# Linear attention: the sample states' stores and row fetches queued behind the small tokens' weight requests, their scaled copies behind an eviction

## Chip, cores and metric

One core of a Trainium2 chip runs the kernel. The metric is the device time of one execution in microseconds (us), as the median of several runs. The engines are PE (TensorE matmuls), PEld (its weight loads), DVE (VectorE), ACT (ScalarE), POOL (GpSimd) and SP (SyncE, which here only issues DMAs).

## What is computed

One inference step of a two-layer trunk: gated linear attention (GLA) with an MLP, then differential attention with an MLP, on 1024 prompt tokens, 16 meta tokens and 8 running sequences with one new token each. The change lies in the first layer, in what the 8 running sequences ("samples") need. For each sample b and each of 4 heads the state of 128 x 256 numbers is updated as

```
q, k, v, lg, r = gla_project(x, w_in, w_gate, b_gate)
new_state = exp(lg)[..., None] * state + k[..., None] * v[..., None, :]
o = q @ new_state
```

and the new states (8 samples of 512 KB) are an output, `gla_state_s`. The samples' and the meta tokens' rows ("small tokens", 24 rows padded to 32) also go through the output projection, the norms, the MLP of layer 1 and the projection of layer 2; the small tokens' results are needed later by the second layer.

## The kernel before

**Prompt.** The projections of the prompt are split-precision matmuls (`mm3`, L205 to L208: three matmuls on high and low parts of both sides). Weights come as 256 KB pieces (`unit`, L191), are cast by ACT (L193, high part) and POOL (L194, low part). For each head h, `proj(h)` (L370 to L392) makes q and k (four accumulations, evicted by ACT at L313/L315) and v (four accumulations, evicted by ACT at L391 into `Y`), `decays` (L435) builds the decay factors with many small ACT (L405 to L407, L419, L420) and DVE (L418, L423, L424) instructions and small matmuls (L452, L467), and `advance` (L494) carries the state from block to block (L500 to L504). While the decays of head 1 are made, PE already works on the projections of head 2.

**Small tokens.** `small_tokens` (L789) is a generator. Each step first uses the two weight tiles of 1 MB that the step before requested (`sload` L234 or `sload2` L240, both from the pool `swt` of two buffers), in 16 matmuls (L722 or L733), and then requests the next two, as soon as the matmuls have freed the buffers. There are 24 such pairs. After the first two pairs, those of the output projection (`gla_w_out`), `s_post` (L736) copies the sums out of PSUM on ACT (L741, "the sums' eviction"), transposes them on PE (L744) and runs a chain of about 15 small operations that ends with the new `sx` (L777); the pairs of the MLP follow, whose matmuls need that `sx`. The function `deal` (L829) advances the generator by one step.

**Sample states.** `state_updates` (L653) is a second generator, with 8 rounds n. In a round, `fetch` (L661) requests a 512 KB broadcast row of v into a part of `Y` (L665) and, for rounds 5 to 7, a 512 KB state (L646); `outer` (L672) scales that row on ACT by k, four instructions (L674); `update` (L667) does decay and sum on DVE, four instructions (L670); `store` (L676) writes the state back (L678). The rows lie in `Y[:, 4096:7168]`, where heads 2 and 3 later put their v.

**Order.** The instructions are not issued in the order of the program text: a planner goes through a simulated timeline and puts on each engine's queue the ready instruction that stands first in the program. The order on each engine is then fixed, and an engine waits in order. `tc.issue_after(x)` makes the instructions inside the block come after x on x's engine; it adds no wait of its own. `swl` is a list of weight requests, which before the change only `sload2` fills; L644 to L646 uses its entry `w_in`. The loop at L834 to L848 advances `updates` by one round after every accumulation of `proj`, and `small` after every second one.

Of the kernel before, what the change touches and what calls it, by code (L numbers as in the profile page):

```python
# [15 lines left out]
AF = mybir.ActivationFunctionType  # L16
# [9 lines left out]
NM = 16  # L26
NS = 8
TS = 32
GH = 4
# [85 lines left out]
def hybrid_step(ctx, tc, A, dbg=None, upto=9):  # L115
    nc = tc.nc
    V, S, G, TE = nc.vector, nc.scalar, nc.gpsimd, nc.tensor
    dma = nc.sync.dma_start
# [23 lines left out]
    def mmt():  # L142
        return banks["mm"].tile([P, 512], F32, name="mmt") if "mm" in banks else pairt()[:, 0]
# [4 lines left out]
    def smt():  # L148
        return banks["sm"].tile([P, 512], F32, name="smt")
# [75 lines left out]
    def s2():  # L225
        return s2p.tile([P, 512], F32, name="s2")

    def swt():
        return swp.tile([P, 2, D], F32, name="swt")

    def sload(src):

        t = swt()
        dma(t.rearrange("p k n -> p (k n)"), src)  # L234
        return t.rearrange("p k n -> p (k n)")

    def sload2(w, k, eng=None):
# [5 lines left out]
    swl = []  # L243
# [99 lines left out]
    ps = smt()  # L343
# [16 lines left out]
    ps = smt()  # L360
# [9 lines left out]
    def proj(h):  # L370
        hi, lo = qku if h == 0 else qk_unit(h)
        hv, lv = (w.rearrange("p (i k n) -> p i k n", i=2, n=P) for w in (hi, lo))
        for c in range(h == 0, 2):
            cs = slice(512 * c, 512 * c + 512)
            for i in range(2):
                ps = mmt()
                for k in range(NB):
                    mm3(ps, hv[:, i, k, :], lv[:, i, k, :], XH[:, k, cs], XL[:, k, cs], k == 0, k == NB - 1)
                evict_qk(c, i, ps)
                yield  # L380
        hi, lo = v0u if h == 0 else kunit(wi, 1024 + h * 256)
        hv, lv = (w.rearrange("p (k n) -> p k n", n=256) for w in (hi, lo))
        for c in range(2):
            for i2 in range(2):
                ps = mmt()
                for i in range(2):
                    t = 4 * c + 2 * i2 + i
                    for k in range(NB):
                        a = slice(t * P, (t + 1) * P)
                        mm3(ps[:, i * 256 : (i + 1) * 256], XH[:, k, a], XL[:, k, a], hv[:, k, :], lv[:, k, :], k == 0, k == NB - 1)  # L390
                S.copy(Yh[:, h, 4 * c + 2 * i2 : 4 * c + 2 * i2 + 2, :].rearrange("p i e -> p (i e)"), ps)  # L391
                yield  # L392
# [37 lines left out]
    def gate_in(h, c):  # L430
        pg = axt()
        TE.matmul(pg, wg[32 * c : 32 * c + 16, h * P : (h + 1) * P], gT[32 * c : 32 * c + 16, :], start=True, stop=True)
        return pg
# [79 lines left out]
    def state_out():  # L513
        h, st = ends.pop()
        dma(A["gla_state_p"][0, 0, h], st)

    def head_end(h, st):
        ends.append((h, st))
        rr = rstd_of(gss[:, h, :], 8, 1.0 / 256, g2)
        G.tensor_tensor(Yh[:, h], Yh[:, h], bc(rr, [P, 8, 256], 2), op=ALU.mult)  # L520
# [42 lines left out]
    ps = smt()  # L563
# [4 lines left out]
    ps = smt()  # L568
# [5 lines left out]
    skT = sqk[:, 128:].rearrange("p (h t) -> p h t", t=TS)  # L574
    V.tensor_scalar(sqT, pv[:, 0], P ** -0.5, None, ALU.mult)
    V.tensor_copy(skT, pv[:, 1])
    ps = smt()
# [15 lines left out]
    ps = smt()  # L593
# [5 lines left out]
    for hh in range(2):  # L599
        ps = smt()  # L600
        for i in range(2):
            h = 2 * hh + i
# [11 lines left out]
    ps = smt()  # L614
# [4 lines left out]
    for s in (8, 4, 2, 1):  # L619
        u = t2()[:, :128]  # L620
        level(sb.rearrange("p h t -> p (h t)"), sqk[:, :128], sqk[:, 128:], u, s, V)
        ps = smt()
# [17 lines left out]
    def slot(i):  # L640
        t = Y[:, 5120 + 1024 * i : 6144 + 1024 * i] if i < 3 else st2[:, i - 3, :]
        return t.rearrange("p (h e) -> p h e", e=256)

    def state_in(b, i):  # L644
        with tc.issue_after(w_in):
            dma(slot(i), A["state_gla"][0, b].rearrange("h d e -> d h e"))  # L646

    for b in range(NS):
        state_in(b, b % 5)
        for h in range(GH):  # L650
            TE.matmul(po[h * TS : (h + 1) * TS, :256], qmk[:, h, b, :], slot(b % 5)[:, h, :], start=False, stop=b == NS - 1)

    def state_updates():  # L653

        todo = ((5, 0), (6, 1), (7, 2), (3, 3), (4, 4), (0, 3), (1, 4), (2, 3))

        def vb(n):
            at = 4096 if n < 2 else 4096 + 1024 * (1, 0, 2)[(n - 2) % 3]
            return Y[:, at : at + 1024].rearrange("p (h e) -> p h e", e=256)

        def fetch(n):  # L661
            b, i = todo[n]
            if b < 3:
                state_in(b, i)
            dma(vb(n).rearrange("p h e -> p (h e)"), A["vs"][b : b + 1, :].broadcast_to([P, D]))  # L665

        def update(n):  # L667
            b, i = todo[n]
            for h in range(GH):
                V.scalar_tensor_tensor(slot(i)[:, h, :], slot(i)[:, h, :], ses[:, h, b : b + 1], vb(n)[:, h, :], ALU.mult, ALU.add)  # L670

        def outer(n):  # L672
            for h in range(GH):
                S.activation(vb(n)[:, h, :], vb(n)[:, h, :], AF.Copy, scale=skT[:, h, NM + todo[n][0] : NM + todo[n][0] + 1])  # L674

        def store(n):  # L676
            b, i = todo[n]
            dma(A["gla_state_s"][0, b].rearrange("h d e -> d h e"), slot(i))  # L678

        last = len(todo) - 1  # L680
        fetch(0)
        outer(0)
        for n in range(last + 1):
            yield
            if n:
                store(n - 1)
                if n < last:
                    fetch(n + 1)
                outer(n)
            update(n)  # L690
            if n == 0:
                fetch(1)
        yield
        store(last)
        yield
# [11 lines left out]
    ps = smt()  # L707
# [28 lines left out]
    def s_post(ps, ln, pool):  # L736

        sev = ps
        if pool is spool:
            sev = s2()  # L740
            S.copy(sev, ps)  # L741
        pt = smt()
        for j in range(4):
            TE.transpose(pt[:, j * P : (j + 1) * P], sev[:, j * P : (j + 1) * P], ident)  # L744

        pv = pt.rearrange("p (j q c t) -> p q c j t", j=4, q=2, c=2)
        z = pool.tile([P, NB, TS], F32, name="sz")
        for c in range(2):
            zc = z[:, 4 * c : 4 * c + 4, :]
            V.scalar_tensor_tensor(zc, sx[:, 4 * c : 4 * c + 4, :], ALPHA, pv[:, 0, c], ALU.mult, ALU.add)  # L750
            V.tensor_tensor(zc, zc, pv[:, 1, c], op=ALU.add)
        s_ln(z, ln, pool)

    def s_ln(z, ln, pool):
        s1 = pool.tile([P, TS], F32, name="ss1")
        V.tensor_reduce(s1, z.rearrange("p k t -> p t k"), op=ALU.add, axis=AX.X)
        pm = smt()
        TE.matmul(pm[:, :TS], inv, s1, start=True, stop=True)
        V.tensor_tensor(z, z, bc(pm[:, :TS], [P, NB, TS], 1), op=ALU.subtract)
        z2 = s2()[:, : NB * TS].rearrange("p (k t) -> p k t", t=TS)  # L760
        V.tensor_tensor(z2, z, z, op=ALU.mult)
        V.tensor_reduce(s1, z2.rearrange("p k t -> p t k"), op=ALU.add, axis=AX.X)
        pm = smt()
        TE.matmul(pm[:, :TS], inv, s1, start=True, stop=True)
        v = pool.tile([P, TS], F32, name="sv_")
        y = pool.tile([P, TS], F32, name="sy_")
        V.tensor_scalar(v, pm[:, :TS], EPS, None, ALU.add)
        S.activation(y, v, AF.Ln)
        S.activation(y, y, AF.Exp, scale=-0.5)

        V.tensor_tensor(v, v, y, op=ALU.mult)
        V.tensor_tensor(v, v, y, op=ALU.mult)
        V.tensor_scalar(v, v, -0.5, 1.5, ALU.mult, ALU.add)
        V.tensor_tensor(y, y, v, op=ALU.mult)
        V.tensor_tensor(z, z, bc(y, [P, NB, TS], 1), op=ALU.mult)
        V.tensor_tensor(z, z, bc(lnp[:, ln, 0, :], [P, NB, TS], 2), op=ALU.mult)
        V.tensor_tensor(sx, z, bc(lnp[:, ln, 1, :], [P, NB, TS], 2), op=ALU.add)  # L777
# [11 lines left out]
    def small_tokens():  # L789
# [35 lines left out]
        dma(A["sxd"], sx)  # L825

    small, updates = small_tokens(), state_updates()

    def deal():  # L829
        next(small, None)  # L830
# [3 lines left out]
    for h in range(1, GH):  # L834
        for n, _ in enumerate(proj(h)):
            if n == 1:
                state_out()
            next(updates, None)
            if n % 2:
                deal()  # L840
        st = SM[:, h, :]
        pgs = [gate_in(h, c) for c in range(2)]
        for c in range(2):
            parts = decays(h, c, pgs[c])
            if c or h == 1:
                deal()
            st = advance(h, c, st, *parts)
        head_end(h, st)  # L848
# [3 lines left out]
    for h in range(GH):  # L852
# [3 lines left out]
        for c in range(2):  # L856
            cs = slice(512 * c, 512 * c + 512)
            sil, pts = [], []
            for m in range(2):
                ps = mmt()  # L860
# [390 lines left out]
    for u, t2_ in ((u, t) for u in range(12) for t in range(4)):  # L1251
# [6 lines left out]
        ps = mmt()  # L1258
        for i in range(2):
            t = 2 * t2_ + i  # L1260
# [139 lines left out]
    ps = smt()  # L1400
# [34 lines left out]
    heads, vals, todo = {0: head}, {0: load_v(0)}, []  # L1435
    steps = [(h, n, t) for h in range(8) for n, t in enumerate((3, 2, 1, 0, 7, 6, 5, 4) if h == 7 else (7, 1, 5, 3, 6, 0, 4, 2))]
    for step in steps + [None] * 0:
        if step:
            h, n, t = step
# [93 lines left out]
    def samples():  # L1533

        sev = s2()
        dma(sev, A["srow"])
        s_post(sev, 2, hp)
        yield
# [282 lines left out]
```

## Time and profile before

| | |
|---|---|
| median of 3 runs | 2797.39 us (2790.05 to 2799.0) |
| the profiled execution's own time | 2801.98 us |
| its span, first to last instruction | 2800.2 us |
| PE busy | 2718.8 us, 97% |
| PEld busy | 2231.4 us, 80% |
| DVE, ACT, POOL busy | 69%, 40%, 38% |
| read from HBM, written | 533.00 MB, 29.52 MB |

The profile shows one execution. "Busy" of an engine counts its instructions, not the waits between them; the time an engine sits idle stands in brackets behind the instruction that ended the idle time, with what released it. PE's instructions overlap a little, and their ends are modelled, so that only its idle times are read here as lost.

### The profile page before, as it was taken

The numbers are of one execution on the slowest core, as the hardware profiler recorded it, in microseconds if no ns is written. First come the engines' busy times: TensorE is split into PE (matmuls) and PEld (weight loads), VectorE is DVE, ScalarE is ACT, GpSimd is POOL, SyncE is SP. The second block draws the span as 40 slices with busy tenths as digits, with TensorE's granted clock in tenths as the row PEclk, the third lists the DMA queues.
The fourth block names the chain that finished last, engine by engine and source line by source line (L and its number), as shares of the span: only waits on it lengthen the run. The fifth ranks groups of instructions, "written<-read, shape, count | busy, mean of one in ns | idle before, by whom it ended". The sixth has DMA issues, their size and how long they took to land. (4 is left out here: it accounts for less than half of the span.)

```text
span 2800.2 us, 52282 instructions
## 1 busy us (share of the span) xinstructions
PE 2718.8 (97%) x19849; PEld 2231.4 (80%) x19849; DVE 1920.3 (69%) x3000; ACT 1125.6 (40%) x2316; POOL 1069.8 (38%) x736
## 2 busy tenths in 40 slices
PE   8999999999999999999999999899999999999998
PEld 5877767987777777777798989777899889798986
DVE  5355453578887777777667730887647878988687
ACT  4354463152231222221242112777626536355554
POOL 2112212334344443434233312200026666676765
PEclk9999999999999999999999999999999999999999
DMA  7575645735898898888658995212144564654575
GB/s 236 166 243 198 216 150 184 262 99 182 294 326 320 313 347 306 329 318 306 252 170 313 366 361 176 66 54 76 35 126 89 104 152 101 144 118 101 137 182 120
DMA packets 276392, 562.81 MB, mean 201 GB/s; under 512 B 23510, under 2 KB 144412, under 8 KB 272044
## 3 DMA queue, kind: packets, MB, share of 16 engines
q1 hardware_dynamic: 256076, 522.75, 54.1%
q0 software_dynamic: 20064, 36.71, 8.1%
q8 instruction: 156, 2.56, 0.4%
q14 instruction: 96, 0.79, 0.1%
HBM read 533.00 MB, written 29.52 MB: 201 GB/s over the span
## 5 line engine op out<-in xcount | busy, mean ns | idle before, releaser
L194 POOL TENSOR_TENSOR wlo<-raw,whi 128x512 fp32r<-128x512 f32 x252 | 365.3, 1463 | 729.1 <-ACT whi L193 643.3
L206 PE MATMUL mmt<-whi,XH 128*128 128x256 f32 (+1 forms) x1760 | 523.9, 300 | 1.1 <-DVE ast L1348 0.9
L207 PE MATMUL mmt<-wlo,XH 128*128 128x256 f32 (+1 forms) x1760 | 521.5, 297 | 0.4 <-POOL wlo L194 0.4
L206 PE MATMUL mmt<-XH,whi 128*128 128x512 f32 (+1 forms) x1216 | 434.5, 359 | 7.2 <-DVE HL L203 2.4
L208 PE MATMUL mmt<-whi,XL 128*128 128x256 f32 x1536 | 432.0, 284 | 0.0
L208 PE MATMUL mmt<-XH,wlo 128*128 128x512 f32 (+1 forms) x1216 | 431.8, 356 | 0.2 <-POOL wlo L1645 0.2
L193 ACT CAST whi<-raw 128x512 fp32r<-128x512 f32 x252 | 150.1, 619 | 567.0 <-PE mmt L208 186.1
L206 PEld LDWEIGHTS mmt<-whi,XH 128*128 128x128 f32 x1760 | 330.2, 188 | 38.8 <-issue 23.5
L953 DVE TENSOR_REDUCE sc<-pg 128x16 f32<-128x1024 f32 x256 | 308.3, 1211 | 68.5 <-POOL pg L952 66.0
L207 PEld LDWEIGHTS mmt<-wlo,XH 128*128 128x128 f32 x1760 | 331.7, 189 | 18.1 <-issue 7.9
L207 PE MATMUL mmt<-XL,whi 128*128 128x512 f32 x768 | 306.7, 400 | 0.0
L952 DVE TENSOR_TENSOR pg<-pg,qb 128x1024 f32<-128x1024 f32 x192 | 265.7, 1391 | 56.7 <-DMA pg<-in_cache_k 49.8
L208 PEld LDWEIGHTS mmt<-whi,XL 128*128 128x128 f32 x1536 | 288.0, 189 | 5.5 <-issue 5.0
L206 PEld LDWEIGHTS mmt<-XH,whi 128*128 128x128 f32 x1216 | 228.8, 189 | 54.3 <-issue 10.8
L952 POOL TENSOR_TENSOR pg<-pg,qb 128x1024 f32<-128x1024 f32 x64 | 162.0, 2533 | 253.8 <-DMA pg<-in_cache_k 159.3
L208 PEld LDWEIGHTS mmt<-XH,wlo 128*128 128x128 f32 x1216 | 229.1, 188 | 34.8 <-issue 2.5
L206 PE MATMUL mmt<-whi,HH 128*128 128x512 f32 x512 | 204.8, 401 | 5.0 <-DVE Y L1185 3.5
L208 PE MATMUL mmt<-whi,HL 128*128 128x512 f32 x512 | 203.9, 398 | 0.0
L207 PE MATMUL mmt<-wlo,HH 128*128 128x512 f32 x512 | 203.4, 397 | 0.0
L1645 POOL TENSOR_TENSOR wlo<-rw,whi 128x512 fp32r<-128x512 f32 x92 | 153.4, 1745 | 88.3 <-ACT whi L1644 88.3
L1645 POOL TENSOR_TENSOR wlo<-RW,whi 128x512 fp32r<-128x512 f32 x96 | 160.5, 1715 | 67.7 <-ACT whi L1644 65.7
L207 PEld LDWEIGHTS mmt<-XL,whi 128*128 128x128 f32 x768 | 145.0, 189 | 38.7 <-issue 7.2
(450 smaller groups left out, 5678.2 us busy)
## 6 DMA issues: line engine op xcount, KB each, us to landing
pg<-in_cache_k SPq DMA_DIRECT2D x256, 512.0 KB
pg<-in_cache_v SPq DMA_DIRECT2D x256, 512.0 KB
raw<-in_mlp_w SPq DMA_DIRECT2D x164, 256.0 KB
swt<-in_mlp_w SPq DMA_DIRECT2D x32, 1024.0 KB
rw<-in_mlp_w SPq DMA_DIRECT2D x116, 256.0 KB
RW<-in_mlp_w POOLq DMA_DIRECT2D x96, 256.0 KB, 5.8
swt<-in_gla_w_in SPq DMA_DIRECT2D x12, 1024.0 KB
swt<-in_diff_w_in SPq DMA_DIRECT2D x12, 1024.0 KB
```

The source lines that it names most:

```text
L193: S.copy(hi[:, c], raw)
L194: G.tensor_tensor(lo[:, c], raw, hi[:, c].bitcast(F32), op=ALU.subtract)
L206: TE.matmul(ps, ah, bh, start=first, stop=False)
L207: TE.matmul(ps, ah, bl, start=False, stop=False)
L208: return TE.matmul(ps, al, bh, start=False, stop=last)
L952: eng.tensor_tensor(pg, pg, qb, op=ALU.mult)
L953: return V.tensor_reduce(sc[:, n, :], pg.rearrange("p (h d) -> p h d", d=64), op=ALU.add, axis=AX.X).ins
L1645: G.tensor_tensor(lo[:, k, :], t, hi[:, k, :].bitcast(F32), op=ALU.subtract)
```

## The change

Three edits. `sload` now also notes its request in `swl`, so that `swl[-1]` is always the latest weight request of the small tokens. In a round of `state_updates` the store and the next fetch are put behind `swl[-1]` on SP, and from the first eviction of `s_post` on, the scaled copies of `outer` are put behind the latest such eviction on ACT. In the loop over the heads `deal` now comes before `next(updates)`.

```diff
     def sload(src):
         t = swt()
-        dma(t.rearrange("p k n -> p (k n)"), src)
+        swl.append(dma(t.rearrange("p k n -> p (k n)"), src).ins)
         return t.rearrange("p k n -> p (k n)")
...
+    evicted = []
+
     def state_updates():
...
         def outer(n):
-            for h in range(GH):
-                S.activation(vb(n)[:, h, :], vb(n)[:, h, :], AF.Copy, scale=skT[:, h, NM + todo[n][0] : NM + todo[n][0] + 1])
+            with tc.issue_after(evicted[-1]) if evicted else nullcontext():
+                for h in range(GH):
+                    S.activation(vb(n)[:, h, :], vb(n)[:, h, :], AF.Copy, scale=skT[:, h, NM + todo[n][0] : NM + todo[n][0] + 1])
...
             if n:
-                store(n - 1)
-                if n < last:
-                    fetch(n + 1)
+                with tc.issue_after(swl[-1]):
+                    store(n - 1)
+                    if n < last:
+                        fetch(n + 1)
                 outer(n)
...
         if pool is spool:
             sev = s2()
-            S.copy(sev, ps)
+            evicted.append(S.copy(sev, ps).ins)
...
             if n == 1:
                 state_out()
-            next(updates, None)
             if n % 2:
                 deal()
+            next(updates, None)
```

## Rows read from the trace of the kernel before

**Rows 1.** The page: span, and busy time of each engine.
```profile
span 2800.2 us, 52282 instructions
PE 2718.8 (97%) x19849; PEld 2231.4 (80%) x19849; DVE 1920.3 (69%) x3000; ACT 1125.6 (40%) x2316; POOL 1069.8 (38%) x736
```
**Rows 2.** Busy time in three stretches: stretch, its length, PE, PEld, DVE, ACT, POOL, clock, DMA.
```profile
0.00:140.00 140.00, 131.78 (x1234) 98.75 (x1235) 64.63 (x154) 59.86 (x145) 26.21 (x24) 0.99 0.62 201
140.00:560.00 420.00, 402.31 (x3773) 314.10 (x3773) 213.25 (x412) 174.00 (x410) 91.48 (x55) 0.99 0.60 209
560.00:2800.00 2240.00, 2184.71 (x14847) 1818.54 (x14845) 1642.43 (x2435) 891.77 (x1761) 952.13 (x657) 0.99 0.63 200
```
**Rows 3.** PE in order of time, 160 to 420 us; idle before and its releaser in brackets.
```profile
162.49 1.92 PE L722 MATMUL smt<-swt,soT 128*32 128x512 f32 x16
180.25 1.92 PE L722 MATMUL smt<-swt,soT 128*32 128x512 f32 x16 [2.44 <-DMA swt<-in_gla_w_out]
189.61 0.91 PE L744 MATMUL smt<-c_ident,s 128*128 128x128 f32 x4 [2.41 <-ACT s L741]
213.84 1.92 PE L733 MATMUL smt<-swt,sx 128*32 128x512 f32 x16
221.77 0.70 PE L501 MATMUL axt<-gS,t 128*128 128x256 f32 x2 [1.67 <-DVE gS L504]
236.92 1.92 PE L733 MATMUL smt<-swt,sx 128*32 128x512 f32 x16 [1.74 <-DMA swt<-in_mlp_w]
283.50 1.92 PE L733 MATMUL smt<-swt,sx 128*32 128x512 f32 x16 [1.28 <-DMA swt<-in_mlp_w]
415.01 1.12 PE L501 MATMUL axt<-gS,t 128*128 128x256 f32 x2 [3.01 <-DVE gS L504]
```
**Rows 4.** SP's DMA issues in order of time, 160 to 230 us.
```profile
160.40 3.28 SPq L665 DMA_DIRECT2D Y<-vs  x2
167.65 0.39 SPq L678 DMA_DIRECT2D out_gla_state_s<-Y  x1
168.13 0.46 SPq L665 DMA_DIRECT2D Y<-vs  x1
168.64 2.06 SPq L240 DMA_DIRECT2D swt<-in_gla_w_out  x2
...
181.78 2.78 SPq L646 DMA_DIRECT2D st<-in_state_gla  x2
184.61 0.97 SPq L234 DMA_DIRECT2D swt<-in_mlp_w  x2
...
214.97 0.34 SPq L234 DMA_DIRECT2D swt<-in_mlp_w  x1
...
227.97 1.20 SPq L234 DMA_DIRECT2D swt<-in_mlp_w  x2
```
**Rows 5.** ACT in order of time, 175 to 223 us.
```profile
175.10 1.71 ACT L674 ACTIVATE Y<-Y,sqk 128x256 f32<-128x256 f32 x4 [5.31 <-DMA Y<-vs]
...
183.74 1.70 ACT L674 ACTIVATE Y<-Y,sqk 128x256 f32<-128x256 f32 x4
...
187.80 1.29 ACT L674 ACTIVATE Y<-Y,sqk 128x256 f32<-128x256 f32 x3
188.99 0.56 ACT L741 COPY s<-smt 128x512 f32<-128x512 f32 x1
...
222.41 0.57 ACT L391 COPY Y<-mmt 128x512 f32<-128x512 f32 x1
```
**Rows 6.** DVE in order of time: the states' updates of two rounds.
```profile
162.63 5.00 DVE L670 SCALAR_TENSOR_TENSOR Y<-Y,ses 128x256 f32<-128x256 f32 x4 [1.56 <-ACT Y L674]
...
188.76 1.67 DVE L670 SCALAR_TENSOR_TENSOR st<-st,ses,Y 128x256 f32<-128x256 f32 x4
```
**Rows 7.** Busy time and granted clock in two stretches around 190 us (columns as rows 2).
```profile
180.00:200.00 20.00, 16.87 (x162) 11.98 (x163) 19.52 (x44) 12.10 (x33) 3.40 (x3) 0.91 1.01 358
190.00:193.00 3.00, 3.00 (x16) 2.22 (x15) 3.00 (x5) 2.44 (x7) 2.45 (x2) 0.50 0.99 404
```

## The prediction, made before the changed kernel was run

> **What bounds the kernel now.** I read the page first. Its list of busy times says that PE is busy for 2718.8 of 2800.2 us, and no other engine for more than 69% [rows 1]. So PE's queue sets the time, and a change elsewhere can gain only what it takes out of PE's idle time, which is 2800.2 - 2718.8 = 81.4 us in all. The second view is the busy time by stretches. The change touches nothing before 140 us, and the small tokens, which it serves, are done by 560 us; in that stretch PE is busy for 402.31 of 420 us [rows 2]. The gain is thus bounded: 17.7 us of idle time, plus what a lowered clock takes from busy time.
>
> The third view is PE in order of time, to see which waits make up these 17.7 us. Two large ones lie next to each other, and both belong to the small tokens [rows 3]. At 180.25 us PE has sat idle for 2.44 us until the second pair of output-projection weights landed. At 189.61 us it has sat idle for 2.41 us until ACT had copied the sums out of PSUM (L741). [...]
>
> The fourth view, SP in order of time, tells why the pair was late. The first pair's matmuls run from 162.49 us for 1.92 us, so the buffers are free at 164.4 us [rows 3]. The request for the second pair leaves SP only at 168.64 us, right behind a store at 167.65 and a row fetch at 168.13 us [rows 4]. That store waited for a state update on DVE, which ran from 162.63 for 5.00 us, until 167.63 us [rows 6]. SP waits in order, so 4.2 us of the pair's delay come from the store in front of it. The fifth view, ACT in order of time, tells why the copy was late: four scaled copies at 183.74 us (1.70 us) and three at 187.80 us (1.29 us) stand in front of it, and it starts at 188.99 us [rows 5], although its matmuls had ended at 180.25 + 1.92 = 182.2 us [rows 3].
>
> **The change, part by part.** *Requests on SP.* Under the new rule sit 7 stores, 6 row fetches and 3 state loads, 16 DMAs; the last store is not under it. None is added or removed. The first of them that matter are the store at 167.65 and the row at 168.13 us: both now come behind the second pair. That pair can leave at about 164.5 us. From request to use it took 180.25 - 168.64 = 11.6 us; a later pair with less beside it took 236.92 - 227.97 = 8.95 us [rows 3, 4]. It lands at 173.5 to 176.1 us by these two, and PE asks for it at 180.25 - 2.44 = 177.8 us. At either end the 2.44 us are gone. I take the whole. What SP holds back in exchange is the stores and rows themselves, which wait for the pair's buffers; nobody on PE waits for a store.
>
> The third pair (184.61 us, behind two state loads that held SP for 2.78 us [rows 4]) also leaves earlier, by up to 2.4 us, but its matmuls at 213.84 us [rows 3] wait for the new `sx`, and with no idle time in front, so I cost it at nothing. If `sx` came so early that the weights were last, the cost would be what the pair is late, 0 to 1.74 us as at 236.92 us [rows 3].
>
> *Scaled copies on ACT.* The rounds from the first eviction on, 3 to 7, now stand behind it: 20 instructions, about 0.43 us each (1.70 for four). Without the seven in front of it the eviction would end at 188.99 + 0.56 - 1.70 - 1.29 = 186.6 us; PE asks for it at 189.61 - 2.41 = 187.2 us, so the 2.41 us go [rows 3, 5]. If only the three at 187.80 us leave, it ends at 188.3 us and 1.1 us of the wait stays: the part is worth 1.3 to 2.41 us, and I take 2.41, since both groups belong to rounds behind the eviction.
>
> *The copies come later, and the updates with them.* Rounds 3 to 5 move into the stretch where DVE is busy for 19.52 of 20 us [rows 7], but two later rounds leave it, at 1.67 us for the four instructions [rows 6]. Net that is one round more, 1.7 us, on DVE and as much on ACT (12.1 of 20 us busy). The cover is PE's work on head 2, which is independent of it. If the cover is gone, PE waits 1.7 us at the decays' small matmuls. In the other direction, ACT is freed of a wait of 5.31 us at 175.10 us for a row [rows 5], so that head 1's decays can start sooner. I cost the two at zero together; the ends are -1.7 (the row that shows PE waiting for a DVE chain is 1.67 us at 221.77 us [rows 3]) and +1.7 us.
>
> *Order of `deal` and `updates`.* It lets the store and fetch of a round see the pair requested in the same step; its cost is within the terms above.
>
> *Clock.* With 4.85 us of idle time gone from 178 to 190 us, PE runs without a break here, and the 1.8 us should come back. [...]
>
> **Sum.** 2.44 + 2.41 + 1.8 = 6.65 us. The profiled execution took 2801.98 us and spans 2800.2 us; it lies 4.6 us above the median of the runs, 2797.39 us. It would take 2795.3 us, and the median becomes 2797.4 - 6.65 = 2790.7 us, or 0.24% less. About 0.3%, 8.4 us, is what a measurement of this kernel can tell from no change: below 2789.0 us is faster, above 2805.8 us slower.
>
> **Rivals.** *More waits go.* The small tokens' chain runs ahead, and with it the later waits for weights, 1.74 us at 236.92 and 1.28 us at 283.50 us, and the 1.67 us for DVE at 221.77 us [rows 3]: 6.65 + 4.69 = 11.3 us, 2786.1 us. With the 3.01 us at 415.01 us, and as much clock as here, 1.8 us, it is 16.1 us, 2781.2 us. For it speaks that ACT's 5.31 us hold in front of head 1's decays goes; against it, that each later pair is requested only when the pair before is used, so that PE's fixed order sets their pace. Chance 0.37.
>
> *The waits only move.* The planner may put the second pair's matmuls, or the transposes behind the eviction, earlier on PE's queue by as much as it believes to gain; then PE meets the same lateness at an earlier place: 2797 us. For it speaks that the order on PE is planned from a simulated timeline which was 2.44 us too hopeful here. Against it, the 4.2 us on SP came from a DVE stretch of 5.00 us where 1.67 us is usual [rows 6], which is more than a plan made from usual durations would allow for. That the change does nothing at all is excluded for this pair by the order on SP; for later pairs it is nearly so, since they already stand ahead of their stores. Chance 0.08.
>
> *ACT waits for rows in a bad place: slower.* The copies of rounds 4, 6 and 7 now need rows that are requested behind a pair of 2 MB. A row requested at 168.13 was used at 175.10 us and held ACT for 5.31 us [rows 4, 5], but ACT had little else to do there. Three such holds, now between the exponentials of head 1's decays and in front of the eviction of head 2's v at 222.41 us (which needs the row's place in `Y`), would be 15.9 us. If PE's cover takes up none of it, the sum is -6.65 + 15.9 = +9.3 us, 2806.7 us. It decides from the point where the request at 214.97 us [rows 4], the fourth pair's, does not move ahead: the sixth and seventh rows then land after 222 us. Against it, PE has two more accumulators free for v before it must stop, and the plan knows the dependence. Chance 0.13.
>
> **Chances and range.** Forecast case 0.42, around 2790.7 us, within 0.3%: from 2789.0 to 2794 us with the copies' lower bound and one round of DVE against it. With the moved waits 0.08, the same side gets 0.50; faster 0.37; slower 0.13. The range goes from the far end of the first rival, 2781 us, up to 2803 us, where the slow rival is half covered by PE's other work; outside stay most of the slow rival and a little below. The forecast case alone is 2789 to 2794 us.
>
> **What would show it.** Right: on SP the second `gla_w_out` pair at about 164.5 us, ahead of the rows; on PE no idle time in front of the second L722 group and of L744; L741 on ACT with no L674 between its matmuls and itself; a granted clock of 1.00 from 180 to 200 us; idle time of PE in 140 to 560 us near 13 us instead of 17.7. Wrong: L674 waiting for rows between the L419/L420 instructions, followed by idle time of PE in front of L452, L467 or L501; or L722 still waiting for `gla_w_out`. A difference that arises after 560 us would mean that the reason is another one altogether.

## The result and the profile after

The changed kernel takes 2799.24 us (median of 22 executions, 2795.34 to 2814.04), the kernel before on the same chip 2794.48 us (22 executions). The ratio is **1.0024, from 1.0015 to 1.0034**: slower by about 7 us, where 0.24% less had been forecast. The ratio is estimated from all executions; the two medians alone differ by 4.8 us. A second set of executions, on another chip, gave 1.0021 (1.0011 to 1.0032), so the sign is settled although the size is under the 0.3% that was called no change.

The profiled execution took 2795.89 us. The page, and busy time by stretches (columns as in [rows 2]):

```profile
span 2794.1 us, 52276 instructions
PE 2718.8 (97%) x19849; PEld 2232.5 (80%) x19849; DVE 1909.2 (68%) x3000; ACT 1128.4 (40%) x2316; POOL 1076.3 (39%) x736
```
```profile
140.00:560.00 420.00, 402.54 (x3752) 314.48 (x3748) 214.51 (x413) 172.82 (x406) 85.80 (x55) 0.98 0.60 209
560.00:2800.00 2240.00, 2182.95 (x14835) 1817.91 (x14833) 1630.20 (x2433) 894.41 (x1761) 964.41 (x657) 0.99 0.63 199
180.00:200.00 20.00, 16.23 (x209) 12.67 (x208) 18.53 (x47) 10.18 (x27) 2.33 (x2) 0.86 0.56 197
194.00:201.00 7.00, 6.12 (x46) 4.82 (x47) 5.30 (x16) 2.17 (x5) 0.00 (x0) 0.52 0.00 0
220.00:240.00 20.00, 17.27 (x294) 15.07 (x293) 13.03 (x29) 11.48 (x32) 2.68 (x2) 0.91 0.81 290
```

In 140 to 560 us PE is idle for 420 - 402.54 = 17.46 us, against 17.7 before [rows 2]. The forecast wanted 13. The clock of 180 to 200 us is 0.86 where it was 0.91 [rows 7], and from 194 to 201 us it is near half.

SP's queue did what the change says. The second pair of output-projection weights now leaves ahead of stores and rows (answering to [rows 4]):

```profile
160.03 1.24 SPq L240 DMA_DIRECT2D swt<-in_gla_w_out  x2
161.32 1.20 SPq L681 DMA_DIRECT2D out_gla_state_s<-Y  x2
162.62 9.50 SPq L667 DMA_DIRECT2D Y<-vs  x2
```

PE in order of time, the waits of the small tokens and of head 2 (answering to [rows 3]):

```profile
169.02 1.92 PE L726 MATMUL smt<-swt,soT 128*32 128x512 f32 x16 [0.78 <-DMA swt<-in_gla_w_out]
175.88 0.60 PE L748 MATMUL smt<-c_ident,s 128*128 128x128 f32 x4
194.31 0.63 PE L768 MATMUL smt<-ss,c_inv 128*128 128x32 f32 x2 [2.41 <-DVE ss L766]
222.33 0.45 PE L467 MATMUL axt<-t 128*32 128x32 f32 x16 [1.10 <-ACT axt L508]
224.87 0.55 PE L206 MATMUL mmt<-whi,XH 128*128 128x256 f32 x1 [1.21 <-ACT Y L391]
279.44 3.60 PE L737 MATMUL smt<-swt,sx 128*32 128x512 f32 x16 [2.16 <-DMA swt<-in_mlp_w]
```

The two waits that the change aimed at are gone or nearly so: 2.44 us became 0.78 us, and the 2.41 us in front of the transposes (L744 before, L748 now) became none. In their place stand waits that were not there: 2.41 us in front of the second statistics product of the norm (L768), 1.10 and 1.21 us in head 2's work near 222 us, and 2.16 us for MLP weights where there were 1.28.

ACT and DVE show what the new waits wait for (answering to [rows 5] and [rows 6]). ACT first:

```profile
171.01 0.59 ACT L745 COPY s<-smt 128x512 f32<-128x512 f32 x1 [0.62 <-PE axt L452]
...
184.22 1.72 ACT L677 ACTIVATE Y<-Y,sqk 128x256 f32<-128x256 f32 x4 [2.36 <-DMA Y<-vs]
...
190.45 1.71 ACT L677 ACTIVATE Y<-Y,sqk 128x256 f32<-128x256 f32 x4 [1.85 <-DMA Y<-vs]
...
224.23 0.59 ACT L391 COPY Y<-mmt 128x512 f32<-128x512 f32 x1 [1.08 <-DVE st L672]
```

And DVE:

```profile
191.29 0.43 DVE L765 TENSOR_TENSOR s<-sz 128x256 f32<-128x256 f32 x1
192.49 1.27 DVE L672 SCALAR_TENSOR_TENSOR st<-st,ses,Y 128x256 f32<-128x256 f32 x3 [0.78 <-ACT Y L677]
193.68 0.58 DVE L766 TENSOR_REDUCE ss<-s 128x32 f32<-128x256 f32 x1
...
222.15 2.78 DVE L672 SCALAR_TENSOR_TENSOR st<-st,ses,Y 128x256 f32<-128x256 f32 x4 [1.19 <-DMA st<-in_state_gla]
```

The squares of the norm (L765) end at 191.72 us. Their sum (L766), for which PE waits, could start then. It starts at 193.68 us, since three state updates stand in front of it on DVE, and the first of them waits 0.78 us for ACT's scaled copies. That is 1.96 of PE's 2.41 us. Near 222 us another round of updates is late, and the eviction of head 2's v (L391) needs the place in `Y` that it reads. Both are **a new clash of the sample states' work with something that PE needs soon**.

The late round near 222 us comes from the rule for the requests itself, by way of the stores. The states of rounds 3 to 7 share two places, so the state of round 6 can be loaded only when round 4's is stored. Two stores stand behind the weight request at 204.21 us, although the updates of rounds 4 and 5 ended at 189.5 and 194.7 us, and the state of round 6 is requested at 215.14 us. SP in order of time:

```profile
204.21 1.20 SPq L234 DMA_DIRECT2D swt<-in_mlp_w  x2
205.46 0.42 SPq L681 DMA_DIRECT2D out_gla_state_s<-st  x1
...
215.14 0.37 SPq L646 DMA_DIRECT2D st<-in_state_gla  x1
```

In the kernel before, two states leave at 181.78 us [rows 4], and the last round of updates is over at 204.4 us, long before head 2's v (DVE):

```profile
202.75 1.66 DVE L670 SCALAR_TENSOR_TENSOR st<-st,ses,Y 128x256 f32<-128x256 f32 x4
```

The profiled execution of the changed kernel reaches this stretch 3.6 us earlier (its last sample product, L651, starts at 150.2 us, that of the kernel before at 153.8 us), so lags are counted from there. The sums' eviction starts 20.8 instead of 35.2 us behind it, 14 us earlier. The norm's result `sx` is complete 49.4 instead of 58.0 us behind it, only 9 us earlier. Some 40% of the lead was given back within the norm.

### The profile page after: what moved, and what is told of

The parts are those of the page before. It is cut to its first block, busy times and chain, and to the rows that moved or that the text cites. A ratio compares the mean times of both kernels' runs of the same rounds, so it can differ in the third digit from the quotient of the medians.

```text
span 2794.1 us, 52276 instructions
## 1 busy us (share of the span) xinstructions
PE 2718.8 (97%) x19849; PEld 2232.5 (80%) x19849; DVE 1909.2 (68%) x3000; ACT 1128.4 (40%) x2316; POOL 1076.3 (39%) x736
```

## The experiments

Three theories stood after the comparison. *Late rows*: copies and updates wait for rows that SP now requests later. *Early matmuls*: with the request ahead, the planner puts the second pair and all that follows it earlier on PE, and PE meets the norm and head 2's eviction before DVE and ACT are ready; the clock falls behind the short waits (0.52 from 194 to 201 us, above). *Late order*: the planner orders the attention of layer 2 anew, far from the change, and that costs the time.

**e1: without the rule for the copies.** The two other edits stay.

```diff
-            with tc.issue_after(evicted[-1]) if evicted else nullcontext():
-                for h in range(GH):
-                    S.activation(vb(n)[:, h, :], ...
+            for h in range(GH):
+                S.activation(vb(n)[:, h, :], ...
```

> The change without its rule on the scaled copies (ACT); the requests on SP are ordered as in the changed kernel. Its plan differs from the changed kernel's in one place only: the sums' eviction comes one copy group later on ACT. Theory 1 (late rows): the changed kernel loses time because the rows of the sample states, now behind 2 MB of weights, reach ACT and DVE late, in the middle of head 1's decays. Then this one is as slow as the changed kernel, 1.0015 to 1.0035 of the kernel before, and L677/L674 again waits 2 to 3 us for rows several times between 170 and 220 us. Theory 2 (early matmuls): PE's order was planned with the norms' small matmuls earlier, and meets them unready; the same order on PE, so the same time, with about 2.4 us of idle time before the second norm matmul. Theory 3 (late order): the time is lost in the attention of layer 2, where the planner also changed PE's order; the same time. If it is instead the rule on the copies that costs, this one is at 0.9985 to 1.0005.

Measured 1.0014 (1.0002 to 1.0026). PE's order is the same as in the changed kernel, and the waits are nearly so: 2.22 us in front of the norm's second statistics product, 1.33 us for L391. The rule for the copies is not what costs the time, or at most a part of it: 1.0014 against 1.0024 and 1.0021, with intervals that overlap. It gains nothing either, since the pair's matmuls now stand so early that the copies no longer lie in front of the eviction.

**e2: without the rule for the requests.** Stores and rows go out when they are ready.

```diff
-                with tc.issue_after(swl[-1]):
-                    store(n - 1)
-                    if n < last:
-                        fetch(n + 1)
+                store(n - 1)
+                if n < last:
+                    fetch(n + 1)
```

> The change without its rule on SP: stores and rows are requested when ready, as before; the copies stay behind the sums' eviction, deal stays in front. Theory 1: no late rows beyond those of before, so 0.998 to 1.0005 of the kernel before; the 2.44 us wait for gla_w_out stays, the 2.41 us wait for the eviction goes. Theory 2: PE's order around the norms stays near that of before, so also about 1.000. Theory 3: the order in the attention of layer 2 is changed here as well, so 1.0015 to 1.0035.

Measured 1.0003 (0.9991 to 1.0016). PE waits for the pair again:

```profile
177.45 1.92 PE L725 MATMUL smt<-swt,soT 128*32 128x512 f32 x16 [2.08 <-DMA swt<-in_gla_w_out]
...
197.05 0.41 PE L767 MATMUL smt<-ss,c_inv 128*128 128x32 f32 x2 [1.95 <-DVE ss L765]
```

The loss is gone with the rule for the requests. The wait in front of the norm's second product is there all the same, 1.95 us, where the wait for the eviction has gone, so that wait alone is not the loss. The wait for L391 is not there. PE's order of the attention in layer 2 is nearly that of the changed kernel, which speaks against the late-order theory; but the first layer of e2's one profile is some 3 us shorter than that of the kernel before, and a late loss of that size could hide behind it.

**e3: only the stores behind the requests.** Rows and states are fetched when they can be.

```diff
                     store(n - 1)
-                    if n < last:
-                        fetch(n + 1)
+                if n < last:
+                    fetch(n + 1)
```

> The change, but only the stores stay behind the weight requests on SP; rows and states are fetched when ready. Theory 1: ACT and DVE no longer wait for rows between 170 and 220 us (under 1 us in all), and the time falls back to 0.998 to 1.0007. Theory 2: the second pair of gla_w_out still comes early and the norms with it, PE still meets them unready: 1.0015 to 1.0035. Theory 3: 1.0015 to 1.0035.

Measured 1.0033 (1.0023 to 1.0044). The kernel is no faster, and PE waits 3.14 us in front of the norm's second product instead of 2.41. But the lateness that the edit should have taken away is still there. PE, DVE and ACT:

```profile
196.07 0.63 PE L768 MATMUL smt<-ss,c_inv 128*128 128x32 f32 x2 [3.14 <-DVE ss L766]
```
```profile
193.84 1.67 DVE L672 SCALAR_TENSOR_TENSOR st<-st,ses,Y 128x256 f32<-128x256 f32 x4 [1.10 <-DMA st<-in_state_gla]
```
```profile
188.37 1.71 ACT L677 ACTIVATE Y<-Y,sqk 128x256 f32<-128x256 f32 x4 [2.88 <-DMA Y<-vs]
```

The update in front of the norm's sum now waits 1.10 us for its state, and ACT waits for rows as long as before. Only the last two rows leave some 20 us earlier; the last two states leave at 214.04 and 215.40 us instead of 215.14 and 217.67, since the stores that free their places are still held back. So e3 shows that fetching freely is not enough. It does not refute the late-rows theory, whose condition, under 1 us of waiting for rows, it did not reach.

**e4: the change once more**, for the scatter of a kernel measured twice.

> The changed kernel again, on the same chip as the three others: 1.0015 to 1.0035 by every theory. Its second profile tells which of the waits of the first come back: theory 1 expects the waits of ACT for rows (2.71, 2.36, 1.85 us) again within 1 us, theory 2 the 2.41 us of PE before the second norm matmul; theory 3 expects the difference to the kernel before to arise after 1700 us.

Measured 1.0021 (1.0011 to 1.0032), with the same waits (2.26 us for the norm, 1.21 us for L391).

**x1: updates behind the norm.** If the early-matmul theory holds, taking the clashes away must bring the forecast gain out. From the first norm on, the updates are put behind the norm's last instruction on DVE.

```diff
+    normed = []
...
-            for h in range(GH):
+            with tc.issue_after(normed[-1]) if normed else nullcontext():
+              for h in range(GH):
...
-        V.tensor_tensor(sx, z, bc(lnp[:, ln, 1, :], ...
+        i = V.tensor_tensor(sx, z, bc(lnp[:, ln, 1, :], ...).ins
+        if pool is spool:
+            normed.append(i)
```

> The changed kernel with one thing more: from the first small-token norm on, the vector engine's state updates are put behind that norm's last instruction, so the norm's reduction can no longer stand behind an update. Early-matmul theory (the small tokens' products now reach TensorE before their operands and the short idles there lower the granted clock): the wait of the norm's statistics product near 194 us (2.41 us in the changed kernel) goes to under 1 us, the half-clock stretch near 195 us (6.8 us long, 3.4 us lost) goes too; together about 5 us less than the changed kernel, ratio to the kernel before 0.9998 to 1.0012. Late-part theory (the time is lost after 560 us): the ratio stays at 1.0015 to 1.0030 although the wait near 194 us is gone.

Measured 1.0008 (0.9994 to 1.0021). The windows' view and PE in order of time:

```profile
180.00:200.00 20.00, 19.37 (x266) 14.20 (x268) 18.36 (x47) 11.62 (x32) 2.81 (x2) 1.00 0.48 179
```
```profile
192.70 0.41 PE L770 MATMUL smt<-ss,c_inv 128*128 128x32 f32 x2 [0.34 <-DVE ss L768]
...
221.42 0.58 PE L206 MATMUL mmt<-whi,XH 128*128 128x256 f32 x1 [1.96 <-ACT Y L391]
```

The norm's wait is 0.34 us, PE is busy for 19.37 of 20 us there and the clock is 1.00. But the wait for L391 grew from 1.21 to 1.96 us, and idle time in 140 to 560 us is still 16.9 us. With one clash removed the other is larger.

**x2: the row of round 6 elsewhere** (rounds counted from 0). The row is placed in the last quarter of `Y[:, 4096:8192]`, so that head 2's v does not need its place.

```diff
-            at = 4096 if n < 2 else 4096 + 1024 * (1, 0, 2)[(n - 2) % 3]
+            at = 4096 if n < 2 else 4096 + 1024 * (1, 0, 2, 1, 3, 2)[n - 2]
```

> The changed kernel, with the value row of the sample states' sixth round put into another quarter of its buffer, so that the copy that wants this quarter back near 224 us need not wait for the updates. Early-matmul theory: the three short idles of TensorE at 222 to 225 us (1.10, 0.42 and 1.21 us) shrink to under 1.5 us in sum and the half-clock stretch near 225 us goes; 3 to 4.6 us less than the changed kernel, ratio to the kernel before 1.0005 to 1.0015. Late-part theory: 1.0015 to 1.0030.

Measured 1.0010 (0.9994 to 1.0025). The windows' view and PE:

```profile
220.00:240.00 20.00, 18.19 (x330) 15.47 (x317) 14.12 (x31) 12.18 (x34) 2.73 (x2) 1.00 0.93 337
```
```profile
194.68 0.41 PE L768 MATMUL smt<-ss,c_inv 128*128 128x32 f32 x2 [2.22 <-DVE ss L766]
...
281.99 3.64 PE L737 MATMUL smt<-swt,sx 128*32 128x512 f32 x16 [3.27 <-DMA swt<-in_mlp_w]
```

The wait for L391 is gone and the clock of 220 to 240 us is 1.00 instead of 0.91. The norm's wait stays, and the one for MLP weights near 280 us grew from 2.16 to 3.27 us. Neither ratio, of x1 or x2 alone, can be told from 1.

**x12: both edits**, twice.

> Both of the edits of the two runs before. Early-matmul theory: the gains add, 8 to 9 us less than the changed kernel; ratio to the kernel before 0.9980 to 1.0003. Late-part theory: 1.0015 to 1.0030.

> The changed kernel with both edits once more, to narrow its interval: both theories have their say already; if the gain of the first time (0.9982, from 0.9966 to 0.9997) is real, the ratio lies between 0.9965 and 0.9995 again, the idle of TensorE between 140 and 560 us near 10 us and the granted clock there at 1.00.

Measured 0.9982 (0.9966 to 0.9997), and 0.9983 (0.9972 to 0.9995) the second time. The second one's windows and its PE:

```profile
140.00:560.00 420.00, 410.39 (x3840) 321.46 (x3839) 216.05 (x423) 178.00 (x413) 88.14 (x57) 0.99 0.60 212
180.00:200.00 20.00, 19.77 (x273) 14.52 (x271) 18.35 (x47) 11.47 (x31) 2.82 (x2) 1.00 0.50 187
```
```profile
170.57 1.92 PE L728 MATMUL smt<-swt,soT 128*32 128x512 f32 x16 [0.42 <-DMA swt<-in_gla_w_out]
...
192.51 0.41 PE L770 MATMUL smt<-ss,c_inv 128*128 128x32 f32 x2
```

PE's idle time in 140 to 560 us is 9.6 us (9.9 the first time) instead of 17.5. Both waits of the kernel before are under half a microsecond, and so are the norm's and head 2's. With the clashes out of the way the same change, together with the two edits, gains some 5 us. The lateness itself is still there: ACT waits 2.71 us for a row at 175.86 us, and the last two states leave at 210.38 and 224.42 us, with a last round of updates that waits 0.94 us for its state. Nothing that PE needs soon stands behind them any more. This speaks for a cost that late rows and states have only where the plan puts something behind them that PE needs.

**b12, n12, m12: is that the change, or the two edits?** The three are the kernel before with both edits, and the changed kernel with both edits less the rule for the requests or less the rule for the copies.

> The kernel before, with the two edits of the run that had both (updates behind the first norm's last instruction; the sixth row in another quarter), and without the change. If the change's gain was there and only hidden by what the planner made of it (early-matmul theory), the two edits alone do not reach it: the wait for the second output-projection pair (2.44 us in the kernel before) stays, the idle of TensorE between 140 and 560 us stays above 13 us, ratio 0.9990 to 1.0020. If the two edits are gains of their own that have nothing to do with the change, the ratio is that of the changed kernel with both, 0.9982, or below, and the idle falls to some 10 us.

> The changed kernel with both edits, but without the rule that puts stores and rows behind the weight requests. Early-matmul theory: the wait for the second pair comes back with about 2 us (2.08 us without this rule in the changed kernel) and no pair comes earlier; ratio 0.9990 to 1.0010. If the rule is of no weight either, the ratio is the 0.9982 of the changed kernel with both.

> The changed kernel with both edits, but without the rule that puts the scaled copies behind the sums' eviction. Early-matmul theory: the rule for the copies is of little weight (leaving it out of the changed kernel gave 1.0014 against 1.0021 to 1.0024), so the ratio is 0.9970 to 1.0000 and the second pair's wait stays under 1 us.

Measured: b12 1.0013 (0.9997 to 1.0029), n12 1.0004 (0.9991 to 1.0018), m12 **0.9973 (0.9962 to 0.9984)**. The windows' view and PE of b12, then of n12, then the windows of m12:

```profile
140.00:560.00 420.00, 398.07 (x3709) 309.60 (x3708) 209.37 (x405) 173.75 (x410) 87.70 (x55) 0.98 0.60 208
```
```profile
179.07 1.49 PE L725 MATMUL smt<-swt,soT 128*32 128x512 f32 x12 [1.97 <-DMA swt<-in_gla_w_out]
...
188.33 0.66 PE L747 MATMUL smt<-c_ident,s 128*128 128x128 f32 x4 [2.25 <-ACT s L744]
```
```profile
140.00:560.00 420.00, 407.69 (x3808) 318.38 (x3807) 219.75 (x422) 173.78 (x411) 87.01 (x56) 0.99 0.61 210
```
```profile
179.08 1.50 PE L728 MATMUL smt<-swt,soT 128*32 128x512 f32 x12 [2.16 <-DMA swt<-in_gla_w_out]
```
```profile
140.00:560.00 420.00, 410.16 (x3864) 323.03 (x3863) 217.12 (x424) 178.60 (x414) 89.84 (x57) 1.00 0.60 212
```

The two edits alone gain nothing (b12 has both old waits and 21.9 us of idle time). Without the rule for the requests the pair's wait is back (n12). So the rule for the requests is worth n12 to x12, 1.0004 to 0.9982 or 0.9983, about 0.21% or 6 us, once nothing stands in the way, and it costs 0.2% (e2 to the changed kernel) when something does. By the intervals each of these two differences is uncertain by some 0.15%; the turn from 1.0024 or 1.0021 to 0.9982 or 0.9983 is well clear of it. n12's profile also shows that an idle time of one execution does not carry 0.2%: it has 12.3 us in 140 to 560 us, less than any profile of the kernel before (16.0 to 17.7 us), and the kernel is no faster. The four cases side by side, as ratios to the kernel before:

| | clashes as they come | clashes removed |
|---|---|---|
| requests not ahead | 1 (before), 1.0003 (e2) | 1.0013 (b12), 1.0004 (n12) |
| requests ahead | 1.0024, 1.0021, 1.0014 (e1) | 0.9982, 0.9983, 0.9973 (m12) |

One rival changes along with the clashes. The planner has two orders for the attention of layer 2 (from the first to the last transposition of L1245, counted in the kernel before). The changed kernel, e1, e2, e3, n12 and x1 have one, or nearly; the kernel before, x2, x12, m12 and b12 have the other, or nearly. The lower right cell thus differs from the lower left one by the late order too. Its price can be read from the profiles: this stretch takes 232.0 to 234.3 us in the nine with the order of the kernel before (mean 233.0) and 232.9 to 235.8 us in the eight with the other (mean 234.2; p8 is left out), some 1.2 us. The first layer's stretch (next table) falls by 9 us from the changed kernel to x12. Of the some 11 us between the two ratios most thus lies in the first layer, and the late order can be about a tenth of it.

**p8: the later part planned anew.** The small load of the page table was issued eight times more ahead of layer 2.

```diff
+    dma(ptab, A["page_table"])
...
```

> The changed kernel, where the small load of the page table ahead of layer 2 is issued eight times more (the same bytes to the same place): the order of the first layer stays as in the changed kernel, that of the later part is planned anew. Early-matmul theory: the first 560 us are as in the changed kernel and the ratio to the kernel before stays at 1.0010 to 1.0030. Late-part theory: the wait for the decode's maximum near 1506 us (2.85 us in the changed kernel) and the clock there come out otherwise, and the ratio moves to 1.0000 or below, or above 1.0035.

Measured 1.0056 (1.0035 to 1.0078), outside the early-matmul theory's range. But the run is not a clean one. PE's order of the attention stayed that of the changed kernel, so the part that was to be changed was not, and between 560 and 650 us PE is idle for 4.4 us against 1.8. It shows that a small edit elsewhere can cost more than this change does; on the question it is inconclusive.

**Four more profiled executions**, three of the kernel before and one of the changed kernel, to see how far one of them can be trusted.

> The kernel before, looked at again for its stage lengths. Early-matmul theory: the stretch from the last sample product to the first transposition of the output rows is commonly 263 to 266 us, shorter than the 267.2 us of the first profile and than the changed kernel's 266.2 to 269.4. Late-part theory: it is 267 us again, and the attention's 232.0 us (233.4 to 235.8 in the changed kernel) comes again too.

> As the look before it: 263 to 266 us by the early-matmul theory, 267 us by the late-part theory; the attention at 232 us by both, if its order by itself makes 1 to 3 us.

> As the two looks before it: 263 to 266 us for the stretch of the first layer by the early-matmul theory, 267 us by the late-part theory.

> The changed kernel looked at again: by both theories the first-layer stretch is 266 to 270 us with a half-clock stretch near 195 us, and the attention 233 to 236 us.

"First-layer stretch" is from the last sample product (L651) to the first transposition of the output rows (L869 in the kernel before). Lost to the clock is the time at half clock in it, halved.

| | first-layer stretch, us | PE idle in it | lost to the clock | attention of layer 2 |
|---|---|---|---|---|
| before, first profile and three more | 267.2, 266.2, 263.9, 264.1 | 15.8, 15.2, 14.1, 14.3 | 3.4, 3.4, 1.7, 1.7 | 232.0, 233.0, 233.9, 234.3 |
| changed: first profile, e4, one more | 269.4, 266.2, 266.5 | 15.6, 13.9, 16.0 | 6.8, 5.1, 3.4 | 233.4, 235.8, 232.9 |
| x12, twice | 258.3, 258.2 | 8.0, 7.7 | 1.7, 1.7 | 232.5, 232.3 |
| m12 | 256.4 | 8.0 | 0 | 232.5 |

By their means the changed kernel's stretch is 267.4 - 265.4 = 2.0 us longer: 15.2 against 14.9 us of idle time, and 5.1 against 2.6 us lost to the clock. The attention's 232.0 us did not come again; it scatters from 232.0 to 234.3 us in one and the same kernel, so the 0.7 us between the means of these kernels shows nothing by itself; over all profiles the two orders lie 1.2 us apart (above).

**What stays open.** Some 2 of the 6 to 7 us are seen in the first layer and about 1 in the order of the attention; where the rest lies is not settled. The profiled executions can't say: from the last transposition of L1120 (L1124 in the changed kernel), near 2130 us, to the end they take 664.7 to 669.8 us before and 660.5 to 663.0 us after, 6 us *less*, in work that the change does not touch, so the profiled executions of the changed kernel are even the shorter ones (2793.7 to 2797.7 us against 2797.8 to 2802.0). Only the timed comparisons carry the sign.

## Why the prediction was wrong, point by point

**Both waits go: right.** The request left at 160.03 us, ahead of the rows, and 1.66 of 2.44 us went (all but 0.39 to 1.32 us in three executions). The eviction follows its matmuls at once, 169.02 + 1.92 = 170.94 and 171.01 us, and its 2.41 us went whole. The end of the range in which only a part of it goes did not come. The reason given for the 2.41 us, the rule for the copies, was not needed: without it (e1) the eviction follows its matmuls at once too, 171.07 + 1.93 = 173.00 and 173.06 us. Nor were the two waits as fixed as the sum took them: in three more executions of the kernel before the pair's was 2.51, 1.46 and 2.12 us and the eviction's 2.41, 2.40 and 0.68 us.

**The size of the gain: not refuted, where nothing takes it back.** The sum was 6.65 us, 0.24%. The rule for the requests measured about 0.21% between n12 and x12, uncertain by some 0.15%. That they agree so closely is luck in part, since n12 already lacks most of the eviction's wait (0.38 us are left).

**Copies and updates "at zero together", with ends of -1.7 and +1.7 us, and "nobody on PE waits for a store": this is the step that failed.** In its place the runs showed new waits of PE: 2.41 us at the norm and 1.21 us at head 2's v, both behind updates, and 1.10 us at head 2 behind ACT, where two rounds of copies now stand between 216 and 221 us. That is 4.72 us in sum, as much as the two old waits, 4.85 us. There are two ways to the first two; that the copies make the third was not tried by itself.

The first is the order. The sum took waits out of a PE order that it held fixed. The order did not stay: the planner, told that the request goes first, put the second pair's matmuls and the norm behind them earlier (counted from the last sample product the pair starts 18.8 instead of 26.4 us behind it, of which 1.7 us is the shorter wait), and DVE's order put updates ahead of the norm's sum. That DVE was busy for 19.52 of 20 us was in front of me [rows 7]; I used it to price one round of updates at 1.7 us, on the decays, and not to ask which small operation of the moved chain would stand behind them.

The second is the held stores. PE does wait for a store, over four links: the store frees the place of a state, the state is loaded late, its update is late, and the eviction of head 2's v waits for the row's place. The third pair, costed at nothing, did cost nothing: its matmuls at 203 us have no idle time in front of them.

**Rival "the waits only move", 0.08: what happened, and too cheap.** It named the right mechanism (PE meets a lateness at an earlier place) with the wrong place: the transposes met none and the pair 0.39 to 1.32 us, the next link of the chain did. My argument against it, that the 4.2 us on SP were an exception, concerned the pair only. It also priced the moved waits at equal cost.

**"The 1.8 us should come back": failed.** They were (1 - 0.91) x 20 us, the loss in 180 to 200 us [rows 7]. The clock there went to 0.86, (1 - 0.86) x 20 = 2.8 us, with half clock from 194 to 201 us (0.52) behind the moved wait, and two further falls near 225 and 280 us (0.91 over 220 to 240 us, 0.88 over 276 to 290 us). In the first-layer stretch the clock cost twice what it cost before, 5.1 against 2.6 us by the means of the table above. With the clashes removed (x12) the clock of 180 to 200 us is 1.00, as forecast.

**Rival "more waits go", 0.37: in part, and without a gain.** The 1.67 us at 221.77 and the 1.74 us at 236.92 us [rows 3] went. The wait for MLP weights near 280 us grew from 1.28 to 2.16 us; the 3.01 us at 415 us [rows 3] became 1.47 us there, beside a new 1.21 us at 411 us. With the clashes removed, though, 9.6 us of idle time were left in 140 to 560 us, 8 us less than before: that rival's ground exists, but not for this kernel.

**Rival "ACT waits for rows", 0.13: right sign, and right in the place.** The eviction of head 2's v is late, as it said, for the place of a row; what was late was a state for DVE and not a row for ACT, and PE lost 1.21 us there, not three holds of 5.31 us. ACT does wait for rows, 2.36 and 1.85 us above, and the second of these makes the update late that stands in front of the norm's sum (0.78 of the 1.96 us). No run took this lateness away by itself, so what rows in time would be worth is not shown.

**"A difference that arises after 560 us" would mean another reason.** Not excluded: about half of the 6 to 7 us could not be placed. That the first layer matters is shown by the timed kernels, where the clashes' removal there turns the loss into a gain, with a first-layer stretch 9 us shorter.

## What to carry to other kernels

A wait that is removed ahead of a chain can hand its time to the next link (here 4.72 us of new waits for 4.85 us of old ones), and where a planner orders the queues it can move the whole chain forward into work that was harmless before. So follow the chain to its end: for each of its operations on a nearly full engine, ask what stands in front of it at the new time, and price those waits before counting the gain. Ask the same of what is held back: a store that nobody waits for can free the place that the next load needs. When a right fix shows no gain, look for the first new wait behind it, take that away too, and compare the four cases; neither of the two further edits had shown a gain by itself.

## What the runs showed of the hardware that was not expected

**The clock's fall is not fixed by the waits.** The first profile of the kernel before and the next two had waits of 2.44 and 2.41, 2.51 and 2.41, and 1.46 and 2.40 us at the pair and the eviction, and clocks of 0.91 [rows 7], 0.83 and 0.91 in 180 to 200 us. So nearly equal waits cost (1 - 0.91) x 20 = 1.8 us in one execution and (1 - 0.83) x 20 = 3.4 us in another, and less idle time cost as much as more. The windows' view of these two:

```profile
180.00:200.00 20.00, 17.31 (x161) 12.51 (x154) 18.87 (x43) 11.87 (x32) 3.04 (x2) 0.83 0.95 340
```
```profile
180.00:200.00 20.00, 17.38 (x174) 12.21 (x166) 19.39 (x44) 12.53 (x33) 3.04 (x2) 0.91 1.02 368
```

Likewise 2.41 us in front of the norm's product are followed by 0.72 over 192 to 204 us in the changed kernel's profile, which is 3.4 us lost, and 2.32 us by 0.83 over 196 to 206 us in its last profile, 1.7 us lost. A fall can also stay away: the changed kernel's wait for MLP weights near 280 us was 2.16, 2.08 and 2.48 us in its three profiles, and the clock over 276 to 290 us was 0.88, 1.00 and 1.00. In these profiles like waits thus cost 1.8 or 3.4 us of clock in the kernel before, and 0 or 1.7 us in the changed kernel.

**A small DVE instruction took 2.31 or 0.22 us.** In the decode near 1500 us the same operation on 8x16 numbers took ten times as long where an operation of POOL had just begun. DVE and POOL of the kernel before, in one execution and then in another:

```profile
1502.72 2.31 DVE L943 TENSOR_SCALAR sc<-own,c_other 8x16 f32<-8x16 f32 x1
```
```profile
1502.61 2.40 POOL L952 TENSOR_TENSOR pg<-pg,qb 128x1024 f32<-128x1024 f32 x1 [6.03 <-DMA pg<-in_cache_k]
```
```profile
1498.97 0.22 DVE L943 TENSOR_SCALAR sc<-own,c_other 8x16 f32<-8x16 f32 x1
```
```profile
1499.21 3.35 POOL L952 TENSOR_TENSOR pg<-pg,qb 128x1024 f32<-128x1024 f32 x1 [5.31 <-DMA pg<-in_cache_k]
```

In the first, POOL starts 0.11 us ahead and both end at about 1505.0 us; in the second, DVE is 0.24 us ahead and POOL's operation is long, 3.35 us. All 18 profiles agree: in the nine where POOL's operation begins 0.01 to 0.18 us ahead, the DVE instruction takes 2.30 to 2.38 us (2.38 in the first profile of the changed kernel, POOL 0.01 us ahead); in the other nine it takes 0.21 or 0.22 us (0.22 in the first profile of the kernel before, POOL 0.57 us behind). What links the two is not shown. Which of the two comes first changes from execution to execution of one kernel, so the 2.3 us are no trace of the change.
